# A two-layer decoder on one core: weight sums in place and one set of banks in the down products, half-width first loads and a third raw buffer in the up products

## The chip, the core and the metric

The kernel runs on one core of a Trainium2 chip. It has five engines with queues of their own: TensorE (PE; its weight loads are listed as PEld) multiplies matrices out of SBUF into PSUM, which has eight banks of 128 x 512 float32; VectorE (DVE) and ScalarE (ACT) work element by element on both memories; GpSimd (POOL) does small work and issues part of the stores; SyncE (SP) issues the loads. Transfers between DRAM and SBUF run on 16 DMA engines. The metric is the time of one execution in microseconds; before the change three runs took 2399.58 to 2401.26 us, the median is 2400.32 us.

## What is computed

A batch of one sequence of 1024 tokens with 1024 features goes through two layers. Layer 0 mixes tokens by latent attention, layer 1 by a gated linear recurrence (HGRN2); each then applies a squared-ReLU MLP with 4096 hidden features. Around each part stands a norm before and after:

```python
def sq_relu_mlp(h, w1, w2):
    a = jax.nn.relu(h @ w1)
    return (a * a) @ w2

# per layer
h = h + rms_norm(mixer(rms_norm(h, gain0)), gain1)
h = h + rms_norm(sq_relu_mlp(rms_norm(h, gain2), w1, w2), gain3)
```

Everything is float32. The change touches the MLP alone: its up part (h @ w1, ReLU, square) and its down part (times w2, the norm after it, and the residual).

## The kernel before

**Products in three multiplies.** TensorE multiplies in a rounded float32 format. To keep the precision each operand is split into a rounded part, which ScalarE makes (line 76), and the rest, which VectorE makes (line 77); a product of two such pairs is three multiplies (lines 81 to 83). So each weight that is loaded costs one ScalarE and one VectorE instruction before TensorE can use it. The split weights `w` stand in five buffers, the raw loads `raw` in two: one in the pool `G0`, one in `G`.

**Seven products for eight.** Both parts of the MLP cut their matrices in 2 x 2 blocks and use the Winograd form of Strassen's method: seven products of sums of blocks in place of eight products of blocks. The sums of weight blocks are made on VectorE from the loaded blocks, and so are the sums of the results.

**Up part (`mlp_up`, from line 703).** The activations lie in SBUF with features on partitions, in blocks B11, B12, B21, B22; four sums of them, T1 to T4, are made once by `tsums` (line 722). The 4096 hidden features are taken in 16 blocks `p` of 256 columns of w1. A block's weights are two raw halves, rows 0 to 511 and rows 512 to 1023 (`raw_half`, line 766), 512 KB each with 1 KB pieces. The first pass (line 849) does for the first eight blocks (`EARLY`) only the two products that need no T, with B11 and B21: it loads both halves and uses 128 of the 256 columns of each, so two splits of 128 x 512; the first product alone (`sP1`) and the hidden block h11 go through two buffers `he` to DRAM (`psp`, `hsp`). It stands ahead of `tsums` and is given priority. The main pass (line 860) loads the halves of each block again, loads h11 and sP1 for the first eight blocks (lines 864, 866), and computes the rest in `others` (line 803): sums of raw weights on VectorE (lines 806 to 810; lines 809 and 810 are the last to read the raw halves), products b, c, d with T2, T1, T3, B22 and T4, sums of results (lines 814 to 831), ReLU and square on ScalarE (lines 784, 785), four sums of hidden blocks (lines 836 to 846), and seven stores to `hsp`, one for each product of the down part. The results stand in tiles `h` and `h2`, taken from two pools by turns: 9 and 4 buffers in layer 0, 6 and 8 in layer 1.

**Down part (`mlp_down`, from line 873).** The 1024 x 1024 output is four quadrants c11, c12, c21, c22, halves of the rows of `y[t]`, eight tiles of 128 tokens. The contraction over hidden features runs in two halves `c`, each with seven products in the order 0, 1, 4, 2, 5, 6, 3. A product has four steps over pairs of hidden blocks `q`: load the hidden pair from `hsp` and split it, take the weight pair (`right(q)`), split it, and multiply into four PSUM banks. The pair of weights for products 4, 2, 5, 6, 3 is made just ahead of its split: line 939 (s11 = b12 - s11), line 1018 (s21 less s22, behind product 2), line 948 (s22 - s11 into a buffer of three, `s12`), line 953 (s22 - b12 into b12), line 957 (s21 + s11). After a product `gather` (line 999) adds the four banks to SBUF tiles: product 0 to U, products 0 and 1 to c11, product 4 to c22, 4 and 2 to c12, 5 to U, 6 to c22, 6 and 3 to c21. Products 0 and 1 use the banks X, 4 and 2 the banks Y, 5 again X, 6 and 3 again Y. In the second half U, which then holds products 0 and 5, is added to c12, c22 and c21 after product 5 (lines 1029 to 1032), the first four tiles are finished in `finish_rows` (line 190: norm, gain `gpost`, residual, store) during product 6, and the last four one after the other as product 3's last steps end (`by_tiles`, line 978, `done`).

**What sets the order.** The program is written in the order above; a planner then orders each engine's queue by its own costs and by priorities, except where `keep_in_program_order` holds an instruction in place: the loads of w2 on SP's queue and the sums of weights on VectorE. Buffers and banks are handed on by semaphores that the planner places. Every engine then works its queue strictly in that order.

## Time and profile before

| | |
|---|---|
| Three runs | 2400.32, 2399.58, 2401.26 us |
| Profiled execution | 2396.59 us, span of the core 2394.9 us |
| TensorE clock granted, mean | 0.987 of full |
| Busy: TensorE, VectorE, ScalarE, GpSimd | 2285.7, 1616.4, 1170.9, 355.5 us |
| DMA | 341.5 MB, 143 GB/s over the span |
| Up part, layer 0 and layer 1 | about 481 to 832 and 1741 to 2066 us |
| Down part, layer 0 and layer 1 | about 832 to 1150 and 2066 to 2395 us |

How to read the lines below. A line of the table of stretches has the start and end of the stretch in us from the span's start, its length, and for each engine the busy us and the number of instructions; then the clock that TensorE was granted (1.00 is full), the mean busy share of the DMA engines and GB/s. A line in order of time has start, length, engine, line of the code, operation, what is written and read, the shape, and in brackets how long the engine had been idle before it and what it waited for. A line of waits has who waited for whom, us in total, how often, and the longest. Matmuls overlap: one of 512 columns is listed with 0.39 us, while the next begins 0.23 us after it. VectorE's instructions also overlap by a little.

### The profile page before, as it was taken

What the parts mean: (1) busy time and instruction counts of PE and PEld (TensorE: products, weight loads), DVE (VectorE), ACT (ScalarE), POOL (GpSimd) and SP (SyncE); (2) the same over time, 40 slices, a digit from 0 to 9 for tenths busy, and PEclk for the clock granted to TensorE, in tenths of its full rate; (3) what the DMA queues carried; (4) which work ended last, traced back from release to release, by engine and by line L of the source; (5) the groups of instructions that cost most, each with busy time, mean ns of one, the idle gap of its engine ahead of it and who ended that gap; (6) DMA issues with size and microseconds to landing.
All of it is one profiled execution on the core that took longest, in us unless ns stands there. A gap on an engine that the chain in (4) does not pass through costs nothing. (4 is left out here: it accounts for less than half of the span.)

```text
span 2394.9 us, 30791 instructions
## 1 busy us (share of the span) xinstructions
PE 2285.7 (95%) x11487; PEld 1918.8 (80%) x11487; DVE 1616.4 (67%) x2311; ACT 1170.9 (49%) x1908; POOL 355.5 (15%) x718
## 2 busy tenths in 40 slices
PE   9999999988899999998899999999978999999996
PEld 8889998866688878886788888888766788888885
DVE  5657884477676557578765667756777767467578
ACT  5445654363344454433575546754453445443443
POOL 1300000121121200001332213221211212100002
PEclk9999999999999999999999999999999999999998
DMA  6000002485554584554612333222455545663743
GB/s 216 27 27 10 10 10 90 157 267 164 172 184 151 187 299 133 190 181 149 219 45 88 106 105 116 83 77 80 150 184 187 200 149 172 214 238 132 257 138 141
DMA packets 229540, 341.51 MB, mean 143 GB/s; under 512 B 16999, under 2 KB 136846, under 8 KB 229390
## 3 DMA queue, kind: packets, MB, share of 16 engines
q1 hardware_dynamic: 205582, 259.84, 33.7%
q0 software_dynamic: 23808, 79.71, 9.0%
q8 instruction: 90, 1.47, 0.3%
q14 instruction: 60, 0.49, 0.1%
HBM read 255.61 MB, written 83.89 MB: 142 GB/s over the span
## 5 line engine op out<-in xcount | busy, mean ns | idle before, releaser
L77 DVE TENSOR_TENSOR w<-raw,w 128x1024 fp32r<-128x1024 f32 (+1 forms) x256 | 280.7, 1102 | 175.9 <-ACT w L76 174.9
L76 ACT ACTIVATE w<-raw 128x1024 fp32r<-128x1024 f32 (+1 forms) x256 | 240.7, 947 | 248.0 <-PE mm L83 82.1
L81 PE MATMUL mm<-A,w 128*128 128x512 f32 x832 | 330.9, 400 | 30.5 <-ACT he L784 12.8
L82 PE MATMUL mm<-A,w 128*128 128x512 f32 x832 | 329.7, 397 | 0.6 <-DVE A L77 0.5
L83 PE MATMUL mm<-A,w 128*128 128x512 f32 x832 | 327.9, 396 | 0.5 <-DVE w L77 0.5
L76 ACT ACTIVATE w<-s 128x1024 fp32r<-128x1024 f32 x156 | 165.1, 1058 | 318.6 <-PE c L83 107.0
L77 DVE TENSOR_TENSOR w<-s,w 128x1024 fp32r<-128x1024 f32 x156 | 190.6, 1222 | 143.2 <-ACT w L76 142.7
L81 PEld LDWEIGHTS mm<-A,w 128*128 128x128 f32 x832 | 158.4, 191 | 72.5 <-ACT he L784 16.1
L145 POOL TENSOR_TENSOR rstd<-rstd,nhalf 128x1 f32<-128x1 f32 x56 | 56.3, 1008 | 964.9 <-DVE rstd L144 939.0
L83 PEld LDWEIGHTS mm<-A,w 128*128 128x128 f32 x832 | 158.7, 191 | 34.2 <-DVE w L77 1.0
L82 PEld LDWEIGHTS mm<-A,w 128*128 128x128 f32 x832 | 158.4, 190 | 33.0 <-DVE A L77 1.4
L82 PE MATMUL mm<-w,w 128*128 128x512 f32 x432 | 171.0, 396 | 12.2 <-DVE w L77 12.2
L781 POOL DMA_DIRECT2D hsp<-h x208 | 112.1, 540 | 467.2 <-ACT h L785 242.6
L83 PE MATMUL mm<-w,w 128*128 128x512 f32 x432 | 169.6, 394 | 0.0
L81 PE MATMUL mm<-w,w 128*128 128x512 f32 x432 | 154.9, 394 | 4.1 <-DVE y L1004 3.2
L81 PE MATMUL mm<-w,A 128*128 128x256 f32 (+2 forms) x352 | 111.1, 318 | 3.6 <-ACT A L76 3.4
L784 ACT ACTIVATE h<-h 128x512 f32<-128x512 f32 x96 | 60.2, 627 | 109.2 <-DVE h L825 70.9
L83 PE MATMUL mm<-w,A 128*128 128x256 f32 (+2 forms) x352 | 111.0, 317 | 0.0
L82 PE MATMUL mm<-w,A 128*128 128x256 f32 (+2 forms) x352 | 110.7, 316 | 0.0
L82 PEld LDWEIGHTS mm<-w,w 128*128 128x128 f32 x432 | 82.1, 190 | 31.2 <-DVE w L77 14.3
L81 PEld LDWEIGHTS mm<-w,w 128*128 128x128 f32 x432 | 81.4, 189 | 24.8 <-ACT w L76 5.7
L81 PE MATMUL c<-T,w 128*128 128x512 f32 x256 | 99.7, 390 | 1.6 <-DVE h L825 1.6
(415 smaller groups left out, 5705.0 us busy)
## 6 DMA issues: line engine op xcount, KB each, us to landing
raw<-in_mlp_w_dram SPq DMA_DIRECT2D x108, 512.0 KB, 4.2
hsp<-h POOLq DMA_DIRECT2D x208, 256.0 KB, 3.1
s<-in_mlp_w_dram SPq DMA_DIRECT2D x80, 512.0 KB, 5.5
raw<-hsp SPq DMA_DIRECT2D x76, 512.0 KB, 4.1
raw<-in_hgrn_w_in_dram SPq DMA_DIRECT2D x64, 512.0 KB, 4.1
sx<-hsp SPq DMA_DIRECT2D x36, 512.0 KB, 4.2
res<-xt POOLq DMA_DIRECT2D x20, 512.0 KB, 4.1
xt<-in_x_dram SPq DMA_DIRECT2D x16, 512.0 KB, 5.7
```

Source lines behind the costliest of these rows:

```text
L76: ACT.activation(dst[:, 0], src, AF.Copy)
L77: DVE.tensor_tensor(dst[:, 1], src, dst[:, 0].bitcast(F32), ALU.subtract)
L81: PE.matmul(ps, lhs[0], rhs[0], start=start, stop=False, skip_group_check=more)
L82: PE.matmul(ps, lhs[0], rhs[1], start=False, stop=False, skip_group_check=more)
L83: PE.matmul(ps, lhs[1], rhs[0], start=False, stop=stop, skip_group_check=more)
L145: POOL.tensor_tensor(r, r, nhalf[:, :1], ALU.pow)
L781: POOL.dma_start(hsp[i, p * P:(p + 1) * P, :], h)
L784: ACT.activation(h, src, AF.Relu)
```

## The change

In the up part:
- The first pass loads one tile per block, all 1024 rows of the 128 columns that it uses (512 KB in 512-byte pieces), and splits it in one 128 x 1024 step for both products.
- The main pass takes its raw halves from three buffers in turn; the third is in the part's own pool, in the place of two tiles `h`.
- The tiles of hidden results come from one ring: the two `he` buffers of the first pass, then 7 `h` and 4 `h2` in layer 0, 4 and 8 in layer 1.

In the down part:
- The sums of weights are made in place, behind the steps of products 2 and 5 (`sums`, `t3`): s11 becomes s22 - s11 and s21 becomes s21 - s11 in product 2's steps, s22 becomes s22 - b12 in product 5's. Products 5, 6 and 3 read s11, s22 and s21. The buffers `s12` now hold loads alone.
- Products 5, 6 and 3 add up in the same four banks, which are read after each: into c12, c22, c21. U holds product 0 alone; in the second half it is added to c12, c22 and c21 right after product 1, and c11's mean square and its gain are done there too.
- The two sets of banks change places in the second half.
- The rows of x for the first four tiles are loaded into s11's buffers, those for the last four into s21's.

```diff
-    def finish_rows(wp, y, ms, gpost, gpre, src, dst, t, xt_bufs=2, xt=None):
+    def finish_rows(wp, y, ms, gpost, gpre, src, dst, t, xt_bufs=2, xt=None, part=slice(0, D)):
...
-        DVE.tensor_tensor(y, y, gpost, ALU.mult)
+        DVE.tensor_tensor(y[:, part], y[:, part], gpost[:, part], ALU.mult)
...
-            new(wp, [P, 512], F32, "h", 9 if layer == 0 else 6)
+            NH, NM = (7, 4) if layer == 0 else (4, 8)
+            new(wp, [P, 512], F32, "h", NH)
...
+            new(wp, [P, 1024], F32, "raw")
...
+            ring = ["he"] * 2 + ["h"] * NH + ["h2"] * NM
             def h512():
+                tag = ring[hs["n"] % len(ring)]
                 hs["n"] += 1
-                if hs["more"] and hs["n"] % 2:
-                    return new(hs["more"], [P, 512], F32, "h2", 4 if layer == 0 else 8)
-                return new(wp, [P, 512], F32, "h", 9 if layer == 0 else 6)
+                p, bufs = {"he": (G, 2), "h": (wp, NH), "h2": (hs["more"], NM)}[tag]
+                return new(p, [P, 512], F32, tag, bufs)
+            def raw_early(p):
+                own["n"] += 1
+                r = new(G0 if own["n"] % 2 else G, [P, 1024], F32, "raw").rearrange("p (k c) -> p k c", c=P)
+                SP.dma_start(r, w1[:, :, p * 256:p * 256 + P])
+                return r
             def raw_half(p, kh):
-                own["n"] += 1
-                r = new(G0 if own["n"] % 2 else G, [P, 1024], F32, "raw").rearrange("p (k c) -> p k c", c=256)
+                hs["r"] += 1
+                r = new((wp, G0, G)[hs["r"] % 3], [P, 1024], F32, "raw").rearrange("p (k c) -> p k c", c=256)
...
-                    rA, rB = raw_half(p, 0), raw_half(p, 1)
-                    a, sP1 = first_two(p, rA, None)
+                    w12 = w_parts(raw_early(p))
+                    a, sP1 = first_two(p, w12[:, :, :4])
                     POOL.dma_start(psp[p * P:(p + 1) * P, :], sP1)
-                    wb = w_parts(rB[:, :, :P])
-                    add_second(p, a, wb)
+                    add_second(p, a, w12[:, :, 4:])
...
-                def t2(q):
-                    t = new(wr, [P, 2, 512], F32, "s12", 3)
-                    tc.keep_in_program_order(DVE.tensor_tensor(t, s22[q], s11[q], ALU.subtract))
-                    return t
+                def sums(q):
+                    tc.keep_in_program_order(DVE.tensor_tensor(s11[q], s22[q], s11[q], ALU.subtract))
+                    tc.keep_in_program_order(DVE.tensor_tensor(s21[q], s21[q], s11[q], ALU.subtract))
                 def t3(q):
                     b12 = load12(q)
-                    tc.keep_in_program_order(DVE.tensor_tensor(b12, s22[q], b12, ALU.subtract))
-                    return b12
-                def t4(q):
-                    tc.keep_in_program_order(DVE.tensor_tensor(s21[q], s21[q], s11[q], ALU.add))
-                    return s21[q]
+                    tc.keep_in_program_order(DVE.tensor_tensor(s22[q], s22[q], b12, ALU.subtract))
...
+                def rows_in(tag, t):
+                    xt = new(wp, [P, 2, 512], F32, tag, KC // 2).rearrange("p a b -> p (a b)")
+                    tc.keep_in_program_order(SP.dma_start(xt, src[t * P:(t + 1) * P, :]))
+                    return xt
...
-                X = four((PG, "mm"), (PG, "tr"))
+                first, second = [(PG, "mm"), (PG, "tr")], [(PM, "mm"), (PM, "c")]
+                if c % 2:
+                    first, second = second, first
+                X = four(*first)
                 product(0, X, first11)
                 gather(U, X)
                 product(1, X, load21, True)
                 gather(c11, X)
-                Y = four((PM, "mm"), (PM, "c"))
+                if last:
+                    for to in (c12, c22, c21):
+                        for t in range(4):
+                            DVE.tensor_tensor(to[t], to[t], U[t], ALU.add)
+                    gpost = row_bcast(wp, "gpost", norm_gains[layer, 3], D)
+                    ms11 = []
+                    for t in range(4):
+                        ms11.append(meansq(c11[t], new(wp, [P, 512], BF16, "junk"), new(wp, [P, 1], F32, f"ms{t}")))
+                        DVE.tensor_tensor(c11[t], c11[t], gpost[:, :512], ALU.mult)
+                Y = four(*second)
                 product(4, Y, t1)
                 gather(c22, Y)
-                def less22(q):
-                    tc.keep_in_program_order(DVE.tensor_tensor(s21[q], s21[q], s22[q], ALU.subtract))
-                product(2, Y, load22, True, less22)
+                product(2, Y, load22, True, sums)
                 gather(c12, Y)
-                X = four((PG, "mm"), (PG, "tr"))
-                product(5, X, t2)
-                gather(U, X, U)
+                X = four(*first)
+                product(5, X, s11.get, after=t3)
+                gather(c12, X, c12)
                 if last:
-                    gpost = row_bcast(wp, "gpost", norm_gains[layer, 3], D)
...
-                        DVE.tensor_tensor(c12[t], c12[t], U[t], ALU.add)
-                        finish_rows(wp, y[t], None, gpost, gpre, src, dst, t, xt_bufs=1 if gpre is not None else 3)
-                        DVE.tensor_tensor(c22[t], c22[t], U[t], ALU.add)
-                        DVE.tensor_tensor(U[t], U[t], c21[t], ALU.add)
-                Y = four((PM, "mm"), (PM, "c"))
-                product(6, Y, t3)
-                gather(c22, Y, c22)
+                        ms12 = meansq(c12[t], new(wp, [P, 512], BF16, "junk"))
+                        finish_rows(wp, y[t], [ms11[t], ms12], gpost, gpre, src, dst, t, xt=rows_in("s11", t),
+                                    part=slice(512, D))
+                product(6, X, s22.get, True)
+                gather(c22, X, c22)
...
-                    product(3, Y, t4, True)
-                    gather(c21, Y)
+                    product(3, X, s21.get, True)
+                    gather(c21, X)
...
-                    product(3, Y, t4, True, n1=2)
+                    product(3, X, s21.get, True, n1=2)
...
-                    by_tiles(3, Y, t4, 0, done, True, lambda: xts.extend(rows_in(4 + t) for t in range(4)))
+                    by_tiles(3, X, s21.get, 0, done, True, lambda: xts.extend(rows_in("s21", 4 + t) for t in range(4)))
```

More of the change, by code (lines that the diff above doesn't have):

```diff
@@ L868, in mlp_up @@
                 else:
-                    a, sP1 = first_two(p, rA, None)
+                    a, sP1 = first_two(p, w_parts(rA[:, :, :P]))
                     wb = w_parts(rB)
@@ L1053, in done @@
                     def done(t):
-                        DVE.tensor_tensor(c21[t], Y[t], U[t], ALU.add)
+                        DVE.tensor_tensor(c21[t], X[t], c21[t], ALU.add)
                         finish_rows(wp, y[4 + t], None, gpost, gpre, src, dst, 4 + t, xt=xts[t])
                         POOL.dma_start(later[t * P:(t + 1) * P, :], y[4 + t])
-                    product(3, Y, t4, True, n1=2)
+                    product(3, X, s21.get, True, n1=2)
                     xts = []
-                    by_tiles(3, Y, t4, 2, done, False, lambda: xts.extend(rows_in(4 + t) for t in range(4)))
+                    by_tiles(3, X, s21.get, 2, done, False, lambda: xts.extend(rows_in("s21", 4 + t) for t in range(4)))
                 else:
@@ L1070, in done @@
                         xt = xts[t]
-                        DVE.tensor_tensor(c21[t], Y[t], U[t], ALU.add)
+                        DVE.tensor_tensor(c21[t], X[t], c21[t], ALU.add)
                         ms = meansq(c21[t], new(wp, [P, 512], BF16, "junk"))
```

9 lines of the change are left out of this document (2 added, 7 removed).

## The prediction

> **What bounds the kernel now.** First the page's busy shares and the table of stretches, to find where TensorE does not run; then the waits and the order of time inside those stretches.
>
> ```profile
> span 2394.9 us, 30791 instructions
> PE 2285.7 (95%) x11487; PEld 1918.8 (80%) x11487; DVE 1616.4 (67%) x2311; ACT 1170.9 (49%) x1908; POOL 355.5 (15%) x718
> ```
>
> TensorE (PE) is busy for 95% of the span, so no other engine can give time except where it makes TensorE stop. The change leaves the matrix multiplies as they are (seven products of the same size); it can only win or lose the stops. The table of stretches shows them (start and end in us, length, then busy us and instructions of each engine, granted clock, DMA):
>
> ```profile
> core 0: us, PE busy (x) PEld busy (x) DVE busy (x) ACT busy (x) POOL busy (x), PEclk, DMA share, GB/s
> 512.90:543.40 30.50, 25.30 (x107) 19.26 (x105) 29.63 (x31) 18.63 (x28) 5.36 (x10) 1.00 0.65 207
> 543.40:663.00 119.60, 104.11 (x425) 82.21 (x426) 80.76 (x115) 45.47 (x63) 19.93 (x37) 0.96 0.53 172
> 663.00:832.00 169.00, 168.31 (x743) 139.04 (x742) 111.57 (x152) 81.55 (x118) 35.60 (x66) 1.00 0.50 171
> 832.00:1091.30 259.30, 258.67 (x1135) 212.37 (x1134) 166.87 (x156) 109.13 (x120) 1.08 (x2) 1.00 0.58 200
> 1091.30:1150.50 59.20, 51.23 (x221) 41.16 (x220) 54.42 (x67) 26.69 (x42) 14.33 (x10) 0.94 0.47 157
> ...
> 1741.00:1785.00 44.00, 34.86 (x137) 26.53 (x135) 35.08 (x37) 23.04 (x38) 7.73 (x15) 0.92 0.59 190
> 1785.00:1905.00 120.00, 107.90 (x452) 86.22 (x452) 84.12 (x120) 48.28 (x66) 20.47 (x38) 0.97 0.55 184
> ...
> 2327.40:2383.00 55.60, 47.75 (x197) 37.86 (x195) 49.61 (x64) 23.15 (x41) 11.06 (x10) 0.94 0.37 129
> 2383.00:2394.90 11.90, 0.22 (x1) 0.00 (x0) 6.82 (x13) 0.72 (x2) 1.65 (x3) 0.61 0.48 177
> ```
>
> The third row is the yardstick: 743 multiplies in 169.0 us, 0.2275 us each, no stop. (The fourth row, layer 0's down products up to product 5 of the second half, has none either.) By it the other stretches lose, counting idle time and half clock together:
> - up, first eight blocks of the main pass (543 to 663 and 1785 to 1905): 119.6 - 425 x 0.2275 = 22.9 us and 120.0 - 452 x 0.2275 = 17.2 us;
> - up, first pass (where I could set a clean edge): 30.5 - 107 x 0.2275 = 6.2 us in layer 0, 44.0 - 137 x 0.2275 = 12.8 us in layer 1;
> - down, products 6 and 3 of the second half (the last two stretches with multiplies): 192 multiplies each, so 43.7 us; 55.6 - 43.7 = 11.9 us in layer 1. Layer 0's stretch has 221 - 192 = 29 more, short transposes, for which I put 4 us: 59.2 - 47.7 = 11.5 us;
> - after the last multiply: 11.9 us.
>
> The seven sums come to 94 us. What causes them, first in the up products (layer 0, then layer 1; waiter, awaited, us in total, times, longest):
>
> ```profile
> DVE s L806 <- DMA raw<-in_mlp_w_dram: 20.7, 7, 4.4
> DVE h L814 <- DMA h<-psp: 8.2, 3, 4.1
> ...
> DVE s L806 <- DMA raw<-in_mlp_w_dram: 19.2, 7, 4.2
> ...
> DVE h L814 <- DMA h<-psp: 3.1, 2, 1.9
> ...
> ACT w L76 <- DMA raw<-in_mlp_w_dram: 12.9, 4, 4.7
> ```
>
> Nearly each of the first eight blocks has VectorE (DVE) waiting some 3 us for raw weights, and TensorE runs dry behind it. The last row is layer 1's first pass: ScalarE, which makes the first part of each split, waits for raw weights there too. In the down products it is VectorE itself. These are TensorE's waits at their places in time, layer 0 then layer 1:
>
> ```profile
> 1109.29 0.80 PE L82 MATMUL mm<-w,w 128*128 128x512 f32 x1 [4.73 <-DVE w L77]
> 1125.13 0.47 PE L81 MATMUL mm<-w,w 128*128 128x512 f32 x1 [3.17 <-DVE y L1004]
> 2346.61 0.80 PE L82 MATMUL mm<-w,w 128*128 128x512 f32 x1 [6.00 <-DVE w L77]
> ```
>
> **Part 1, down: the weight sums and the adds of U.** VectorE's load per product of layer 1's second half (products 1, 2, 5, then 6):
>
> ```profile
> 2240.00:2262.00 22.00, 22.00 (x99) 18.22 (x98) 13.45 (x14) 8.05 (x8) 0.00 (x0) 1.00 0.85 313
> 2284.00:2305.80 21.80, 21.80 (x97) 17.78 (x96) 16.86 (x17) 8.05 (x8) 0.00 (x0) 1.00 0.36 121
> 2305.80:2327.50 21.70, 21.70 (x97) 17.98 (x96) 16.58 (x17) 8.04 (x8) 0.00 (x0) 1.00 0.54 180
> 2327.50:2349.30 21.80, 15.63 (x62) 12.22 (x61) 21.80 (x32) 10.14 (x19) 8.53 (x5) 0.90 0.19 65
> ```
>
> VectorE has 5 to 8 us free in each product until product 6, where it is full for all 21.8 us and TensorE gets only 15.6. So the question is how much work leaves that stretch. Its order of time gives the price of one instruction, as the distance of two starts:
>
> ```profile
> 2329.90 0.68 DVE L1029 TENSOR_TENSOR y<-y,u 128x512 f32<-128x512 f32 x1
> 2330.50 0.68 DVE L1031 TENSOR_TENSOR y<-y,u 128x512 f32<-128x512 f32 x1
> ...
> 2335.85 1.22 DVE L77 TENSOR_TENSOR w<-raw,w 128x1024 fp32r<-128x1024 f32 x1
> 2336.98 1.22 DVE L953 TENSOR_TENSOR s<-s,s 128x1024 f32<-128x1024 f32 x1
> ```
>
> A 512-wide one takes 0.60 (2330.50 - 2329.90), a 1024-wide one 1.13 (2336.98 - 2335.85). Out of products 6 and 3 go: the twelve adds of U (lines 1029, 1031, 1032), 12 x 0.60 = 7.2; half of the four multiplications by gpost (line 199), 4 x 0.53 = 2.1; the four sums of product 3 (line 957), 4.5; and of product 6's (line 953) the two that still fell behind 2327 (2336.98 above is one), 2.3. Together 16.1. VectorE's 49.6 us in the last two products become 33.5, against 43.7 of multiplies; in layer 0 54.4 becomes 38.3 against 47.7. TensorE is the bound again in both. I take back 8 of the 11.5 and 9 of the 11.9 us, leaving some for the first factors of product 3. Bounds: nothing, and 11.5 and 11.9.
>
> Where it goes: the adds and four half gpost multiplications (16 x 0.60 = 9.6) become ready in product 1, whose stretch had 22.0 - 13.45 = 8.5 free; 1 us runs over into product 4, which needs its own first split only. gpost is loaded two products earlier, and its wait on SP's queue stands before nothing that is due. The four mean squares on ScalarE move too; it is busy for 8 of 22 there. Product 2 gets one sum more per pair of blocks: 16.86 + 4 x 1.13 = 21.4 of 21.8, which is the tightest place (rival B). Product 5 loses the sums into a temporary and keeps those of product 6: 16.6 as now. Without this cover each us would stand before TensorE as it does in product 6 now. In all, one 1024-wide instruction per pair goes, sixteen in the kernel, 18 us of VectorE.
>
> The rows of x for the first four tiles now come into s11's buffers, so their four loads on SP's queue wait for product 5's last splits; behind them stand product 6's loads of hidden values. These have three buffers of their own to run ahead with and the splits of product 5 are done by then in any case; I cost it at nothing, and if the cover is gone it is one load per layer, some 4 us. Swapping the pairs of PSUM banks with the half costs nothing: the pair taken was read out a whole product before.
>
> **Part 2, down: one pair of banks for products 5, 6 and 3.** Product 6 used to begin in the other pair; now its first multiply must wait until VectorE has read product 5's sum out of that bank. This happens four times. Nearest rows: the 3.17 us at 1125.13 above is just such a wait with VectorE behind; and the stretch 832 to 1091, which holds five such hand-overs (0 to 1, 4 to 2, 6 to 3 of the first half, 0 to 1 and 4 to 2 of the second), idles for 259.30 - 258.67 = 0.6 us in all. The four banks are read out in turn, one per 0.60 us, while a bank's turn on TensorE is 3 x 0.2275 = 0.7 us long, so it is nearer to the second row: 0.5 each, +2 us in all. Behind the waiting multiply stands all of product 6, as TensorE works in order. Bounds: 0 and 4 x 3.17 = 12.7.
>
> **Part 3, down: the end.** Now all four last tiles end within 5 us, as the last factor's split came late; so VectorE works their ends off one after the other:
>
> ```profile
> 2378.72 0.69 DVE L1071 TENSOR_TENSOR y<-mm,u 128x512 f32<-128x512 f32 x1 [5.55 <-PE mm L83]
> 2382.83 0.39 PE L83 MATMUL c<-wx,w 128*128 128x512 f32 x1
> 2384.40 0.69 DVE L1071 TENSOR_TENSOR y<-c,u 128x512 f32<-128x512 f32 x1
> 2389.13 1.41 DVE L1077 SCALAR_TENSOR_TENSOR s<-y,rstd,s 128x512 f32<-128x512 f32 x2 [0.73 <-POOL rstd L145]
> ```
>
> The last tile's add starts 1.2 us after its multiply is over (2382.83 + 0.39) and its result leaves 7.3 us after (2390.5). With tiles 5.4 us apart it would need about 5: the add, ScalarE's mean square, the root, two multiply-adds. Estimate -2 us, bounds 0 and -4.
>
> **Part 4, up: third raw buffer and one ring for the hidden tiles.** The order of time on VectorE in layer 0's third and fourth blocks:
>
> ```profile
> 555.90 0.68 DVE L810 TENSOR_TENSOR s<-raw,s 128x512 f32<-128x512 f32 x1
> ...
> 562.03 0.69 DVE L806 TENSOR_TENSOR s<-raw,raw 128x512 f32<-128x512 f32 x1 [2.56 <-DMA raw<-in_mlp_w_dram]
> ...
> 563.85 0.68 DVE L807 TENSOR_TENSOR s<-s,raw 128x512 f32<-128x512 f32 x1
> ...
> 565.05 0.68 DVE L810 TENSOR_TENSOR s<-raw,s 128x512 f32<-128x512 f32 x1
> ...
> 572.24 0.69 DVE L806 TENSOR_TENSOR s<-raw,raw 128x512 f32<-128x512 f32 x1 [3.98 <-DMA raw<-in_mlp_w_dram]
> ```
>
> Line 810 frees the second raw buffer; the next line 806 starts 562.03 - 556.58 = 5.5 and 6.5 us later, all of it the load. With three buffers the next block's first half is there already, and its second half takes the buffer of this block's first half, which line 807 frees, 1.2 us before line 810; it also no longer shares the DMA engines with a twin. So 1.2 us of each wait goes for sure and up to all of it (3 us); I take 1.5 x 7 = 10 on VectorE. One load now stands one place further ahead on SP's queue, before the loads of the first pass's values (line 866); rival C prices that. The hidden tiles come from one ring of 13 (layer 0) or 14, where layer 0's smaller pool of four, used every other time, came round after the 8 that one block takes; that shortens the second row of waits. TensorE gets a little less than VectorE does: -8 and -7 us. Bounds: 0 and the whole 22.9 + 17.2 = 40.1.
>
> **Part 5, up: the first pass.** Eight loads of 512 KB instead of sixteen per layer (16 less in all), and one 1024-wide split for two 512-wide. VectorE's price is 1.13 for 2 x 0.60, the same. In layer 0 VectorE was full, 29.63 of 30.5 us, mostly with the T sums, which stay: -1. In layer 1 it was not (35.08 of 44), and loads were waited for 12.9 us: -4. The first product of the pass now waits for the wide split: 1.22 - 0.69 on VectorE and as much on ScalarE, 1 us per layer: +2. Bounds: +2, and -6.2 - 12.8 = -19.
>
> The pieces of such a load shrink from 1024 to 512 bytes. Rows of the DMA issues (KB each, median us to landing):
>
> ```profile
> raw<-in_mlp_w_dram SPq DMA_DIRECT2D x108, 512.0 KB, 4.2
> raw<-in_hgrn_w_in_dram SPq DMA_DIRECT2D x64, 512.0 KB, 4.1
> ```
>
> The second row is three quarters loads of 128 columns, the new shape, and lands no later: price 0. The Trainium skill (DMA: Bandwidth & Descriptors, Why small descriptors are slow) speaks against smaller pieces: a fixed overhead of about 3 cycles on each packet, whose bytes pass 32 at a time. By it two packets of 512 take 2 x (16 + 3) = 38 cycles for 35, an estimated 9% of at most 4.2 us, for 16 loads 6 us if nothing hid it; the sum would be -29. The rows show no such cost at landing.
>
> **The sum**: -8 - 9 + 2 - 2 - 8 - 7 - 1 - 4 + 2 = -35 us. The profiled execution took 2396.59 us, 3.7 below the median of the three runs shown; 2396.6 - 35 = 2361.6, and with the 3.7 the forecast is 2365 us.
>
> **Rivals.**
> - A, only the down half pays: the second half of the raw weights still gates line 806 and VectorE's T sums the first pass. For it: one of the two loads of a block still waits for line 807. Against it: the 5.5 and 6.5 us above are longer than a 4.2 us landing, so loads crowd each other. Parts 4 and 5 give 0: 2400.3 - 17 = 2383.
> - B, only the up half pays: in the second half of the contraction VectorE's backlog moves from product 6 to products 2 and 5, as 21.4 of 21.8 us leaves no room, and stops TensorE there as at 2346.61. For it: that sum. Against it: what waits in product 2 is not due until product 5. Parts 1 and 3 give 0: 2400.3 - 18 + 2 = 2384.
> - C, slower. One mechanism: U (line 814) late in each of the first eight blocks. It adds sP1, loaded by line 866 on SP's queue; one raw load more stands waiting for its buffer ahead of it, and with U go X5, h12, h21, h22. It was late already 5 times, 11.3 us, longest 4.1. If it is late by w in all 16 blocks, parts 4's -15 is gone and 16 w - 11.3 comes on top; against the other -20 it decides from 16 w = 31.3, w = 2.0 us. At the longest seen, 4.1: -20 + 54 = +34, 2434. Against it: the queue's order follows when loads are due, and the hidden tiles' ring is longer.
> - D, no change that can be told: A's reason in the up products and B's in the down ones together, 2400.
> - E, more: all losses of the first table but the hand-over and half of the end: -40 - 19 - 23 + 2 - 2 = -82, 2318; half way from the forecast to it, -58, is 2342.
>
> **How the numbers follow.** The forecast and what is near it (2350 to 2378) 0.52, A 0.18, B 0.10, E 0.07, D 0.07, C 0.06. About 0.2% (4.8 us) is what a measurement can tell from no change. Faster: the forecast, A, B and E, 0.87; same 0.07; slower 0.06. The range leaves out C, most of D and the far end of E: 2343 to 2393.
>
> **What would show it.** Part 1: in products 6 and 3 of the second half VectorE under 40 busy us, and no wait of TensorE over 1.5 us for a split there; the stretch about 45 us long in layer 1. Part 2: waits of TensorE for the read-out at product 6's start, by their length. Part 3: starts of the last tiles' adds about 5 us apart. Part 4: the waits of line 806 for raw weights at half of 20.7 and 19.2 or less. Part 5: 92 loads into raw from the MLP weights where there were 108; the first pass of layer 0 as long as before, that of layer 1 some 4 us shorter. It is wrong if VectorE is full in products 1 and 2 and TensorE waits at product 4 or 5, or if line 814 waits longer for its load than now.

## The result and the profile after

The changed kernel takes 2346.91 us (2346.48 to 2349.69, four runs) beside 2400.79 us before (2399.58 to 2405.72): the ratio is 0.9774, interval 0.9757 to 0.9791. The forecast was 2365 in a range of 2343 to 2393, so the time fell by 54 us where 35 were expected. The profiled execution took 2346.75 us.

The page of the changed kernel: span, busy time, and its first row of DMA issues.

```profile
span 2345.1 us, 30698 instructions
PE 2266.8 (97%) x11487; PEld 1910.8 (81%) x11487; DVE 1596.5 (68%) x2287; ACT 1169.4 (50%) x1893; POOL 346.9 (15%) x718
...
raw<-in_mlp_w_dram SPq DMA_DIRECT2D x92, 512.0 KB, 4.3
```

TensorE issues as many multiplies as before; the span is 49.8 us shorter. VectorE has 19.9 us less to do (18 were forecast), and 92 raw loads stand where 108 were. The median of all of them lands in 4.3 us, with 4.2 before. The table of stretches of the changed kernel, the same places as in the prediction (first pass and main pass of layer 0, down products 6 and 3 of layer 0, first pass and main pass of layer 1, products 2, 5, then 6 and 3 of layer 1, the end):

```profile
core 0: us, PE busy (x) PEld busy (x) DVE busy (x) ACT busy (x) POOL busy (x), PEclk, DMA share, GB/s
512.90:543.40 30.50, 25.54 (x109) 19.75 (x108) 28.24 (x28) 16.07 (x25) 5.37 (x10) 1.00 0.37 128
543.40:663.00 119.60, 114.97 (x504) 93.90 (x503) 93.37 (x133) 52.73 (x74) 23.55 (x44) 1.00 0.63 211
1074.70:1121.10 46.40, 45.97 (x219) 37.85 (x218) 38.20 (x50) 25.69 (x40) 8.11 (x12) 1.00 0.47 159
1711.00:1757.30 46.30, 35.04 (x149) 27.30 (x148) 34.81 (x35) 24.90 (x39) 9.45 (x16) 0.93 0.39 136
1757.30:1877.30 120.00, 115.86 (x492) 94.24 (x493) 93.07 (x133) 51.69 (x72) 22.21 (x42) 0.97 0.60 202
...
2248.00:2269.60 21.60, 21.60 (x96) 17.48 (x95) 21.60 (x22) 11.97 (x12) 0.00 (x0) 1.00 0.45 152
2269.60:2291.30 21.70, 21.70 (x98) 17.96 (x97) 19.17 (x20) 8.21 (x9) 0.00 (x0) 1.00 0.73 236
...
2291.30:2336.30 45.00, 44.96 (x199) 36.91 (x197) 33.41 (x48) 16.74 (x31) 8.30 (x11) 1.00 0.46 171
2336.30:2345.10 8.80, 0.00 (x0) 0.00 (x0) 2.87 (x5) 0.72 (x2) 0.55 (x1) 0.78 0.23 85
```

By the yardstick of 0.2275 us for a multiply the main passes now lose 119.6 - 504 x 0.2275 = 4.9 us (22.9 before) and 120.0 - 492 x 0.2275 = 8.1 us (17.2); products 6 and 3 of layer 1 lose nothing (45.0 - 199 x 0.2275 is below zero; before, the prediction put 11.9 for 192 multiplies, and by the 197 of its row it was 55.6 - 197 x 0.2275 = 10.8). The first passes lose 5.7 and 12.4 us (6.2 and 12.8): as good as nothing came from there.

Waits of the changed kernel, first eight blocks of layer 0, then of layer 1:

```profile
DVE s L818 <- DMA raw<-in_mlp_w_dram: 5.9, 5, 2.1
...
DVE h L826 <- DMA h<-psp: 5.0, 3, 2.7
...
DVE s L818 <- DMA raw<-in_mlp_w_dram: 9.5, 6, 4.1
...
PE tr L81 <- ACT w L76: 5.4, 1, 5.4
...
DVE h L826 <- DMA h<-psp: 1.5, 2, 1.1
```

Line 818 is the former line 806: its waits for raw weights fell from 20.7 to 5.9 and from 19.2 to 9.5 us. Line 826 (formerly 814), which rival C needed to be later, waits less. Longer is one wait of TensorE in layer 1, at its first multiply with a T: 5.4 us, with 2.3 before.

Both executions have the same 11487 multiplies, so the start of the n-th multiply, measured from the first, can be laid beside that of before, stage by stage (us; worked out from the two traces):

```
multiplies       stage                                      forecast  change
    0 -  2900    attention, first pass of layer 0              0        +0.4
 2900 -  3520    main pass, layer 0                           -8       -17.4
 3520 -  5250    down, layer 0, up to product 5               +1        +0.4
 5250 -  5600    down, products 6 and 3, start of layer 1     -8       -10.5
 5600 -  8600    recurrence of layer 1                         0        -3.0
 8600 -  8990    first pass of layer 1                        -3        -3.0
 8990 -  9540    first T multiply, main pass of layer 1       -7        -5.2
 9540 - 11250    down, layer 1, up to product 5               +1        +2.7
11250 - 11480    down, products 6 and 3                       -9       -11.3
                 after the last multiplies                    -2        -2.9
                 sum                                         -35       -49.8
```

### The profile page after: what moved, and what is told of

It reads as the page before. It is cut to its first block, busy times and chain, and to the rows that moved or that the text cites. A ratio compares the mean times of both kernels' runs of the same rounds, so it can differ in the third digit from the quotient of the medians.

```text
span 2345.1 us, 30698 instructions
## 1 busy us (share of the span) xinstructions
PE 2266.8 (97%) x11487; PEld 1910.8 (81%) x11487; DVE 1596.5 (68%) x2287; ACT 1169.4 (50%) x1893; POOL 346.9 (15%) x718
## 3 DMA queue, kind: packets, MB, share of 16 engines
q1 hardware_dynamic: 205326, 251.45, 33.4%
## 5 line engine op out<-in xcount | busy, mean ns | idle before, releaser
L76 ACT ACTIVATE w<-raw 128x1024 fp32r<-128x1024 f32 (+1 forms) x240 | 237.8, 997 | 239.2 <-PE mm L83 119.6
L145 POOL TENSOR_TENSOR rstd<-rstd,nhalf 128x1 f32<-128x1 f32 x56 | 44.4, 794 | 959.1 <-DVE rstd L144 934.2
L794 POOL DMA_DIRECT2D hsp<-h x177 | 95.4, 540 | 388.8 <-ACT h L798 208.7
L81 PE MATMUL c<-T,w 128*128 128x512 f32 x256 | 99.6, 389 | 0.0
L82 PE MATMUL c<-T,w 128*128 128x512 f32 x256 | 99.6, 389 | 0.0
L83 PE MATMUL c<-T,w 128*128 128x512 f32 x256 | 99.3, 389 | 0.0
L81 PEld LDWEIGHTS mm<-w,w 128*128 128x128 f32 x432 | 80.8, 188 | 22.6 <-ACT u L1015 2.9
```

Source lines behind the costliest of these rows:

```text
L76: ACT.activation(dst[:, 0], src, AF.Copy)
L81: PE.matmul(ps, lhs[0], rhs[0], start=start, stop=False, skip_group_check=more)
L82: PE.matmul(ps, lhs[0], rhs[1], start=False, stop=False, skip_group_check=more)
L83: PE.matmul(ps, lhs[1], rhs[0], start=False, stop=stop, skip_group_check=more)
L145: POOL.tensor_tensor(r, r, nhalf[:, :1], ALU.pow)
L794: POOL.dma_start(hsp[i, p * P:(p + 1) * P, :], h)
```

## The experiments

Each is the changed kernel with the edit shown, unless it says otherwise. One kernel's timed runs spread by some 5 us, so differences of 3 us are read in the traces, by the n-th multiply as above, and these are single executions. How far a stage differs between kernels that are the same in it: eight kernels with the changed kernel's up part in layer 0 lie between -16.0 and -18.8 us in that layer's main pass.

**Half of the change at a time.** The first kernel has the down part (`mlp_down`, `finish_rows`) of before, the second the up part of before.

> The up products as changed, the down products as before. From the two traces, multiply for multiply, the up products gained 17 us in layer 0 and 8 us in layer 1. If the two halves of the change are independent: 2400.8 - 25 = 2376 us. If part of the up gain needs the down part (VectorE or the loads starting earlier in layer 1): above 2380. If the down part gains less once the up part has gone ahead: no sign of it here, but up alone would be below 2372.

Measured: 2375.09 us (2372.38 to 2378.03), ratio 0.9910, interval 0.9890 to 0.9929.

> The down products as changed, the up products as before: two pools by turns with the sum P1 outside them, two raw buffers, the old first pass. If the two halves of the change add up: 2399 - 28 = 2371 us (28 is what the kernel with the up part alone left). Beside the kernel with one ring of the same 13 and 14 hidden tiles and two raw buffers (2367.8): theory (the ring pays only by the two buffers that join it) the two agree within 3 us; rival (its order pays by itself) this one is slower by 5 us or more.

Measured: 2374.95 us (2372.86 to 2379.20), ratio 0.9912, interval 0.9892 to 0.9932. In the profiled spans each half gains some 24 us (2370.7 and 2371.1 for 2394.9), 48 together; the whole gains 49.8. But these two executions were the shortest of the four that each half ran. By the timed runs the halves fall short: 0.0090 + 0.0088 = 0.0178 where the whole has 0.0226, some 11 us less, of which the three intervals leave about 8 to noise. So the halves weigh the same, and part of the gain seems to need both. The trace has a place for it: the kernel with the up half alone is 4.8 and 2.3 us slower than before in products 6 and 3 of the two layers (5250 to 5600 and 11250 to 11480), whose code it shares with before. (The second theory of the down kernel is taken up below.)

**The third raw buffer.** The waits of line 818 had fallen as forecast, so I put the gain of the main pass down to them. This kernel has no third raw buffer; its room goes back to two tiles `h`.

```diff
-            NH, NM = (7, 4) if layer == 0 else (4, 8)
+            NH, NM = (9, 4) if layer == 0 else (6, 8)
-            new(wp, [P, 1024], F32, "raw")
-                r = new((wp, G0, G)[hs["r"] % 3], [P, 1024], F32, "raw")...
+                own["n"] += 1
+                r = new(G0 if own["n"] % 2 else G, [P, 1024], F32, "raw")...
```

> The changed kernel without the third raw buffer: raw halves by turns in two, its place back as two hidden tiles (rings of 15 and 16). My theory, that the third buffer takes away VectorE's waits for raw weights in the main pass (20.7 and 19.2 us before, 5.9 and 9.5 after): these waits return to about 20 each, and some 18 of the 25 us of the up products go: 2365 us. Rival, that the single ring of hidden tiles did it, by freeing SP's queue: the waits stay under 10 each and the time under 2352.

Measured: 2344.96 us (2342.42 to 2346.59), ratio 0.9779, interval 0.9763 to 0.9795: no loss. Its waits for raw weights in layer 0 (535 to 690 us), and its stretch of the main pass:

```profile
DVE s L817 <- DMA raw<-in_mlp_w_dram: 19.4, 10, 4.0
```

```profile
543.40:663.00 119.60, 115.83 (x502) 95.17 (x502) 95.06 (x137) 55.50 (x79) 24.47 (x46) 0.99 0.65 216
```

VectorE waits for raw weights as it did before the change (20.7 us), and TensorE still gets 502 multiplies done against 504, where before the change it got 425. The waits that I quoted were VectorE's own and were covered. My theory fell: with two tiles more in its place, the third raw buffer isn't needed. What it is worth beside a ring of the same length is taken up below.

**The ring.** Here the third raw buffer stays, and the tiles come from the two pools by turns again, without the two `he`:

```diff
-                tag = ring[hs["n"] % len(ring)]
                 hs["n"] += 1
-                p, bufs = {"he": (G, 2), "h": (wp, NH), "h2": (hs["more"], NM)}[tag]
-                return new(p, [P, 512], F32, tag, bufs)
+                if hs["more"] and hs["n"] % 2:
+                    return new(hs["more"], [P, 512], F32, "h2", NM)
+                return new(wp, [P, 512], F32, "h", NH)
```

> The changed kernel with the hidden tiles taken from two pools by turns as before (7 and 4, 4 and 8 buffers, the first pass's two left out of it); third raw buffer kept. My theory: the ring is the smaller part, 5 us: 2352 us. Rival, that the ring did it: 2365 us or more, and SP's waits for stores of hidden tiles at the loads of h11 and sP1 back at some 29 us in layer 0's main pass.

Measured: 2354.72 us (2348.33 to 2360.74), ratio 0.9820, interval 0.9796 to 0.9845: nearer to the theory's time. Then the kernel without a third raw buffer, its ring less the two `he`: as many tiles (13 and 14) and raw buffers as before the change, in one ring.

```diff
-            ring = ["he"] * 2 + ["h"] * NH + ["h2"] * NM
+            ring = ["h"] * NH + ["h2"] * NM
```

> The changed kernel without the third raw buffer and without the first pass's two buffers in the ring: 13 hidden tiles in layer 0 and 14 in layer 1, the same pools and numbers as in the kernel before (9 and 4, 6 and 8), but taken in one ring and not by turns. Theory after the first runs, that the order of the ring is the cause (by turns, layer 0's four tiles come round after 8 tiles, one block): as fast as the changed kernel, 2345 to 2349 us. Rival, that the two more buffers are: like the run by turns, 2353 to 2357 us. SP's waits for stores at the loads of h11: theory under 15 us, rival about 26.

Measured: 2367.80 us (2367.50 to 2368.56), ratio 0.9867, interval 0.9853 to 0.9882: above what either side expected. The stretches of the two kernels, the turns first, then the ring of 13 and 14 (layer 0):

```profile
543.40:663.00 119.60, 111.11 (x462) 88.98 (x461) 85.65 (x121) 48.55 (x67) 20.95 (x39) 0.96 0.57 189
```

```profile
543.40:663.00 119.60, 113.88 (x484) 91.29 (x485) 91.80 (x132) 49.44 (x70) 23.20 (x43) 0.99 0.61 203
```

The table lays the kernels side by side by the n-th multiply. A block takes eight tiles; in a pool of four that is used every second time a tile comes round after 8, in one ring after as many as it has. "Depth" is the smaller such number:

```
                       raw   depth    main pass, us against before
                             L0 / L1     layer 0    layer 1
before                  2     8 / 12        0          0
turns (no ring)         3     8 /  8       -6.2       -1.2
ring, without he        2    13 / 14      -12.7       +6.2
changed kernel          3    13 / 14      -17.4       -5.2
ring with he            2    15 / 16      -18.4       -3.0
```

In layer 0 the depth brings most. The kernel with turns differs from the changed one by the ring alone (and by the two `he` that it takes in), and loses 11.2 us here (-6.2 for -17.4). With as many tiles and as many raw buffers as before, the ring and the new first pass bring 12.7 of the 17.4 us; the other 5 or 6 come from the two recruited `he` buffers, and it is the same whether they are tiles themselves or give their room to a raw buffer. So the third raw buffer is not shown to be worth nothing: at the same depth the kernel with three is better by 4.7 us (13), and by 6.2 (8, where the first pass and the down part differ too); two more tiles do as much. Beside the spread of 2.8 us between equal kernels these 5 us are the less certain part. What goes with the depth is a direct wait for a store out of the tile that comes round. The rows of before and, after it, of the kernel with turns (535 to about 690 us):

```profile
ACT h L784 <- DMA hsp<-h: 5.0, 1, 5.0
...
DVE h L814 <- DMA hsp<-h: 2.2, 2, 1.2
```

```profile
ACT h L797 <- DMA hsp<-h: 3.1, 1, 3.1
...
DVE h L837 <- DMA hsp<-h: 1.0, 1, 1.0
```

The three kernels with a ring have no such row in layer 0. These waits come to 7.2 and 4.1 us and are ScalarE's and VectorE's; that they make up the whole gain is not shown. SP's waits for stores at the loads of h11 and sP1, by which two of the expectations wanted to tell, do not go with the time: 29.2 us before, 26.4 with turns, 4.9 with the ring of 13, and 45.8 with the ring of 15, which loses nothing. In layer 1 depth does not order the rows: the ring of 14 with two raw buffers is slower than the turns of before. Why stays open (VectorE waits for such a store there again, 3.3 us); beside it the two `he` buffers are worth 9 to 11 us there. So against the kernel with the down half alone, which has the turns of before, the ring of the same size gains 7 us in the whole (0.9867 for 0.9912), as that kernel's rival theory said. The new first pass stands beside the ring in this comparison, and the gain comes only through layer 0.

**The first pass.** Both halves loaded and split apart, as before the change.

```diff
-                    w12 = w_parts(raw_early(p))
-                    a, sP1 = first_two(p, w12[:, :, :4])
+                    rA, rB = raw_early(p, 0), raw_early(p, 1)
+                    a, sP1 = first_two(p, w_parts(rA[:, :, :P]))
...
-                    add_second(p, a, w12[:, :, 4:])
+                    add_second(p, a, w_parts(rB[:, :, :P]))
```

> The changed kernel with the first pass as before: two full-width halves loaded per block and two 512-wide splits. My theory, that VectorE's T sums set when the main pass can start: hardly a loss, 1 us: 2348 us, the first multiply with T within 1.5 us of where it is now. Rival, that sixteen loads fewer matter (DMA share 0.90 in the first pass before): 8 to 10 us lost, 2356 us.

Measured: 2350.15 us (2346.24 to 2352.00), ratio 0.9800, interval 0.9782 to 0.9817, between the two. In the trace its first pass of layer 1 is 4.4 us shorter than the changed kernel's (-7.4 for -3.0 by the n-th multiply), but the recurrence just ahead is 3.7 us longer. Counted from the start of layer 1 to the first multiply with a T (5600 to 8991), 3.9 us are gained for 3.0, within the theory's 1.5, and TensorE's wait there is about as long as in the changed kernel:

```profile
PE tr L81 <- ACT w L76: 5.1, 1, 5.1
```

Its main pass of layer 0 is 2 us longer, less than the spread, and 6 us go at one wait of 5.0 us in layer 0's first down products. The new first pass brings nothing that these runs can tell.

**The down products: load, or place?** First the load: 27 adds of 128 x 512 into U, which nothing reads any more, 16.2 us of VectorE, put behind product 5 in the second half.

```diff
+                if last:
+                    for i in range(27):
+                        DVE.tensor_tensor(U[i % 4], c12[i % 4], U[i % 4], ALU.add)
                 product(6, X, s22.get, True)
```

> The changed kernel with 27 more adds of 512 columns on VectorE (into U, which nothing reads any more) behind product 5 in each layer's second half, 16.2 us, what the change took out of products 6 and 3 by my sum. They wait for product 5's result as the old adds did. Theory, that VectorE's load there was the whole cause: TensorE's stop in product 6 comes back at 5 to 6 us with some 2 to 4 us of half clock, 11 us per layer: 2368 us. Rival, that the place of the sums or the banks did it: the adds find room, under 2353 us.

Measured: 2354.88 us (2354.02 to 2359.24), ratio 0.9812, interval 0.9795 to 0.9828. Less than half of the expected loss, yet above the rival's 2353. Then the place, twice: the twelve adds of U and the whole gain back behind product 5,

```diff
-                    for to in (c12, c22, c21):
-                        for t in range(4):
-                            DVE.tensor_tensor(to[t], to[t], U[t], ALU.add)
...
+                        DVE.tensor_tensor(c12[t], c12[t], U[t], ALU.add)
+                        finish_rows(wp, y[t], None, gpost, gpre, src, dst, t, xt=rows_in("s11", t))
+                        DVE.tensor_tensor(c22[t], c22[t], U[t], ALU.add)
+                        DVE.tensor_tensor(c21[t], c21[t], U[t], ALU.add)
```

> The changed kernel with the twelve adds of U and the whole gain of the first four tiles back behind product 5; the weight sums stay in place and early. It puts 7.2 + 2.1 = 9.3 us of VectorE back into products 6 and 3. Theory, that VectorE's load against 43.7 us of multiplies decides: VectorE goes from 33 to 42 us there, near full in product 6, and TensorE stops again for some 3 to 6 us per layer: 2353 to 2359 us. Rival, that the early weight sums alone removed the stop: within 2 us of the changed kernel.

Measured: 2347.88 us (2347.02 to 2353.68), ratio 0.9789, interval 0.9773 to 0.9804: the rival's time. And the weight sums, in place but each just ahead of its split:

```diff
-                product(2, Y, load22, True, sums)
+                product(2, Y, load22, True)
...
-                product(5, X, s11.get, after=t3)
+                product(5, X, t2)
...
-                product(6, X, s22.get, True)
+                product(6, X, t3, True)
```

> The changed kernel with the same weight sums, in place, but made just ahead of each split in products 5, 6 and 3 (and x's rows for the first four tiles in buffers of their own, since s11 is still read in product 3). It puts 2.3 + 4.5 = 6.8 us of VectorE back into products 6 and 3. Theory of the load: VectorE at some 40 of 43.7 us, a loss of 0 to 4 us in all: 2347 to 2351 us. Rival, that the point is to have the sums a product ahead: TensorE waits at the start of products 6 and 3 in every half, 8 us or more in all, 2355 us.

Measured: 2354.63 us (2352.79 to 2356.72), ratio 0.9812, interval 0.9797 to 0.9827: the rival's time again. Then both of these in one kernel:

> Both undoings in one kernel: the weight sums in place but made just ahead of their split, and the twelve additions of U with the whole gain back behind product 5; the banks, the end of the last tiles and the up products stay as changed. Alone they cost 1 us (the additions) and 8 us (the sums). Theory (VectorE's second half holds one stop that opens only when the load and the late sums come together): 2370 to 2376 us, as where the down products are all as before (2375). Rival (the two costs add, and the rest of the down gain is the banks' and the end's): 2354 to 2359 us.

Measured: 2363.12 us (2358.88 to 2364.26), ratio 0.9857, interval 0.9838 to 0.9876: between the two. Products 6 and 3 of layer 1 by the n-th multiply (11250 to 11480), against before:

```
down part as changed (eight kernels)   -11.2 to -11.4
adds of U late                         -10.4
weight sums late                        -7.2
27 adds more                            -6.4
adds and sums late                      -1.4
```

Eight kernels with the changed down part and different up parts agree to 0.2 us, so this stage can be read closely. Stretches of product 3 with the 27 adds, and of products 6 and 3 with both late:

```profile
2308.00:2330.00 22.00, 17.83 (x78) 13.91 (x77) 22.00 (x32) 7.81 (x13) 5.82 (x4) 1.00 0.60 216
```

```profile
2296.90:2352.30 55.40, 48.68 (x198) 38.38 (x196) 48.73 (x63) 23.60 (x41) 10.74 (x11) 0.94 0.40 138
```

The 27 adds first fill what VectorE had free: 45.0 - 33.41 = 11.6 us in the changed kernel's products 6 and 3. By this sum only the rest, 16.2 - 11.6 = 4.6 us, can reach TensorE, and 4.9 were lost (11.3 - 6.4). I read that as the load by itself. The late sums cost 4.1 us with far less load, 6.8 us by the expectation, which the 11.6 could have held: a factor whose sum stands just ahead of its split is late by both. TensorE's one longer stop in that kernel is for such a split:

```profile
2314.07 0.50 PE L82 MATMUL mm<-w,w 128*128 128x512 f32 x1 [1.93 <-DVE w L77]
```

VectorE is busy without a gap around it (25.00 of the 25.0 us from 2305), so this run does not part place from load cleanly. Together with the late adds they cost 9.9, more than the 0.9 + 4.1 of each alone, as the adds stand ahead of the sums on a queue that is by then full (48.73 of 55.4, while 198 x 0.2275 = 45.0 are TensorE's). TensorE's waits in that kernel are at the places of before, two for splits and one for the read-out:

```profile
2311.54 0.50 PE L82 MATMUL mm<-w,w 128*128 128x512 f32 x1 [1.40 <-DVE w L77]
2320.80 0.79 PE L82 MATMUL mm<-w,w 128*128 128x512 f32 x1 [3.49 <-DVE w L77]
2329.50 0.47 PE L81 MATMUL mm<-wx,w 128*128 128x512 f32 x1 [1.08 <-DVE y L1020]
```

So in layer 1 load and place bring 9.9 of the 11.3 us. In layer 0 (5250 to 5600) the four kernels of the table lose 3.2, 6.6, 6.8 and 10.6 us against the changed one, where the eight with the changed down part lie between -9.9 and -11.9: with both late nothing is left of the 10.5, and there the two costs simply add. But the fair comparison for that kernel is the one with the up half alone, which has the same up part; it is slower than before at these places, so beside it there are 15.3 and 13.6 us to explain. In the whole load and place are 0.0083 of 0.0136 (the ratios of this kernel and of the up half against 0.9774); the rest is open, the banks among it, which no run here varied by themselves.

**A version with that wait filled.** TensorE's 5.4 us at the first T multiply of layer 1 are about one block of first products, 24 multiplies. The edit for nine blocks there (ten alike):

```diff
-EARLY = 8
+EARLY = (8, 9)
...
-                if p < EARLY:
+                if p < EARLY[layer]:
```

> Nine blocks in the first pass of layer 1 in place of eight, layer 0 as changed: TensorE has one more block of first products (some 5 us) where it now waits 5.4 us at the first product with T. Theory (VectorE's T sums are what it waits for, and the block covers them): 4 to 5 us less than the changed kernel, 2342 to 2343 us. Rival (the block's own weight rounding queues behind the T sums on VectorE, so the wait stays or moves): within 1.5 us of the changed kernel, 2346 to 2349 us.

Measured: 2341.37 us (2340.13 to 2344.12), ratio 0.9772, interval 0.9751 to 0.9793; before ran at 2396.95 us beside it.

> Ten blocks in the first pass of layer 1, layer 0 as changed. Theory: no more than with nine (the wait is 5.4 us, one block's length), 2342 to 2344 us. Rival as with nine: 2346 to 2350 us.

Measured: 2344.45 us (2342.58 to 2347.04), ratio 0.9783, interval 0.9766 to 0.9801.

With nine blocks the wait is gone, first eight blocks of layer 1:

```profile
PE tr L81 <- ACT w L76: 0.7, 1, 0.7
```

By the n-th multiply first pass and main pass of layer 1 (8600 to 9540) gain 8.4 us more with nine (-16.6 for -8.2), the span is 2339.3 us. The ratio doesn't tell it from the changed kernel's; the trace does, at the place, though what follows in the down products gives about 3 us of it back. Ten bring no more.

## Why the prediction was right, and where it was not

**What bounds the kernel.** Right: the change moved only stops of TensorE, and the seven sums that came to 94 us are now 4.9 + 8.1 + 5.7 + 12.4 + 0 + 0 + 8.8 = 40, a difference of 54 beside a span 49.8 us shorter.

**Part 1, down, -8 and -9.** Right in mechanism, a little small: -10.5 and -11.3, nearly all of both losses. VectorE has 33.4 us in layer 1's products 6 and 3, where 33.5 was worked out. But load was only one of two causes. The step that left out the other is the sum "Together 16.1": it priced instructions, while that the sums leave the place just ahead of a split is worth 4.1 us alone in layer 1 and 6.6 in layer 0, and more beside a full queue.

**Product 2 as the tightest place (rival B).** VectorE is full there (21.60 of 21.60; 21.4 was forecast), and TensorE stops nowhere in it. What spoke against B held: nothing made there is due before product 5.

**Part 2, hand-over, +2.** At the new hand-over, from product 5 to 6, TensorE waits in neither layer. The one wait for a read-out, 0.4 us in layer 0, is at the start of product 3, and so was the 3.17 us at 1125.13 from which the bound was taken: there product 3 followed product 6 in the same banks before the change too. +2 was too much.

**Part 3, the end, -2.** The number is right, -2.9, and the last three adds now lie 5.4 us apart, in order of time on VectorE:

```profile
2325.42 0.69 DVE L1084 TENSOR_TENSOR y<-mm,y 128x512 f32<-128x512 f32 x1
...
2330.86 0.69 DVE L1084 TENSOR_TENSOR y<-c,y 128x512 f32<-128x512 f32 x1 [0.43 <-PE c L83]
...
2336.30 0.69 DVE L1084 TENSOR_TENSOR y<-c,y 128x512 f32<-128x512 f32 x1 [0.99 <-PE c L83]
...
2339.33 1.41 DVE L1090 SCALAR_TENSOR_TENSOR s<-y,rstd,s 128x512 f32<-128x512 f32 x2 [0.73 <-POOL rstd L145]
```

But the kernel with the up half alone, whose down part is that of before, is 2.5 us shorter there too, with its last two adds 3.2 us apart:

```profile
2358.28 0.67 DVE L1081 TENSOR_TENSOR y<-c,u 128x512 f32<-128x512 f32 x1
...
2361.52 0.69 DVE L1081 TENSOR_TENSOR y<-c,u 128x512 f32<-128x512 f32 x1 [0.57 <-PE c L83]
```

So the runs bear out that the end depends on how far apart the last tiles come; that the change to the down part is what it takes, they don't show.

**Part 4, main pass, -8 and -7.** Layer 1 was near (-5.2), layer 0 half of what came (-17.4), and most of the miss of the forecast lies here. The failing step is "1.5 x 7 = 10 on VectorE ... TensorE gets a little less than VectorE does". It took VectorE's waits for raw weights for TensorE's stops; without the third buffer, but with two tiles more, these waits are all back and TensorE loses nothing. The sentence on the ring named the right mechanism, tiles that come round after the 8 of one block, and gave it no price of its own: it is worth 11 to 13 us in layer 0. In layer 1 a ring of the size of before brought nothing (+6.2), so that its -5.2 lies near the forecast is luck in part.

**Part 5, first pass, -3 in all.** Layer 0 came as forecast (nothing). In layer 1 -3.0 us stand at the forecast's place, but they are lost again at the next multiply, the first with a T: it waits 5.4 us for a split of a sum that stands behind the T sums on VectorE, and behind it the stage is back at 0.0. The old first pass comes to the same wait. The step on layer 1, "it was not" full and so -4, didn't ask what VectorE owes at the end of the pass. The smaller pieces cost little or nothing at landing: the loads of the new shape landed in 5.3 us at the median, as far as the trace has their landing, those of the old first pass beside the same kernel in 5.1. The price of 6 us estimated from the Trainium skill (DMA: Bandwidth & Descriptors, Why small descriptors are slow) did not show in the time of the first passes; in layer 0's first pass the DMA share fell from 0.65 to 0.37.

**The rivals.** A and B failed by the halves, which both pay; C by line 826, which waits less; D by the result. The measured time lies near half way from the forecast to E, where the prediction had put 2342.

**Not forecast.** 3.0 us less in layer 1's recurrence and 2.7 more in its first down products, both in stages where little changed; the second is not there with the two raw buffers and the longer ring (-0.6), so I read neither as an effect.

## What to carry to other kernels

A wait is worth what the bounding engine loses behind it: before pricing a wait of a helper engine, look for the wait of the bounding one that follows from it. Where tiles come from two pools by turns, the small pool can set how far the producer runs ahead, as it did in layer 0; work out after how many takes a buffer comes round, and try one ring for pools of different size. When an engine overflows at one place, price both its load, less what is free there, and the order of what stands just ahead of the instruction that is due.

## What the hardware showed

A stop of TensorE can cost more than its length. The kernel with both undoings waits 1.40 + 3.49 + 1.08 = 6.0 us in products 6 and 3, but loses 55.4 - 198 x 0.2275 = 10.4 (9.9 beside the changed kernel): after the 3.49 us a multiply takes 0.79 us, and the stretch is granted 0.94 of the clock. The 2.84 us stop of the kernel with 27 adds did not do that:

```profile
2326.00 0.47 PE L81 MATMUL mm<-wx,w 128*128 128x512 f32 x1 [2.84 <-DVE y L1017]
```

The Trainium skill (TensorE: Matmul & The Clock Gate, What's actually happening) gives half rate after an idle window of about 3.4 us; the two rows agree with it. They do not fix the length, as other stops differ: the prediction's row at 1125.13 stood 3.17 us and went on at 0.47, the kernel with the old first pass has one of 4.23 us in layer 1 that was followed by a multiply of 0.50, and the changed kernel has one of 2.17 us, ahead of its T multiplies, that was followed by one of 0.70.

```profile
1798.78 0.50 PE L81 MATMUL mm<-A,w 128*128 128x512 f32 x1 [4.23 <-DVE h L833]
...
1733.60 0.70 PE L81 MATMUL mm<-A,w 128*128 128x512 f32 x1 [2.17 <-ACT he L797]
```
